# A layer's mixture of experts: each slot's step onto the sum moved behind the next slot's up, and two arms in place of four

## The chip, the cores and the metric

One core of a Trainium2 chip runs the whole layer in one launch. The metric is device time in microseconds (us) from one execution; the kernel before took 1340.64 us as the median of three runs (1333.01 to 1342.6).

## The reference

The layer takes x (256 tokens by 2048, float32). A mixer (dilated attention beside a gated recurrence) and a layer norm come first; the change does not touch them. Then come 32 experts, of which each token visits two, and a second layer norm:

```python
p_grp = jax.nn.softmax(xf @ grp_w + grp_b, axis=-1)          # 4 groups, the best one
...
top_v, top_i = lax.top_k(jax.nn.softmax(e_logits, axis=-1), TOP_K)   # its 2 best of 8 experts
weights = g_gate * top_v / jnp.sum(top_v, axis=-1, keepdims=True)
...
def expert_block(args):
    xblk, e = args
    return (jax.nn.silu(xblk @ w1[e]) * (xblk @ w3[e])) @ w2[e]
...
out = jnp.zeros((T + 1, D), x2d.dtype).at[buf_tok].add(yb * buf_w[:, None])
...
x = _layer_norm(ALPHA * x + moe, ln2_g[layer], ln2_b[layer])
```

w1 and w3 of an expert are 2048 by 512, w2 is 512 by 2048, all float32: 12 MB an expert. Experts that no token chose need not be read.

## The kernel before

The mixer takes the first 435 us. Then the routing is computed on the chip, the tokens are sorted by expert into a transposed copy (`xs`), and the experts run one after the other in 32 *slots*. Slots 0 and 1 are experts 0 and 1, whose weights are fetched before the routing is known. The other slots are filled by rank: `RHO[i]` says at which rank of token count slot `i` stands, and `bound(i)` the most tokens that a rank can have. With this data 28 experts have tokens, so slots 0 to 27 run; each is put under `tc.If(n_all > RHO[i])`. The first 25 slots (`TAIL`) are written in one loop, the others in nested conditions at the end, with the statistics of the layer norm behind each add.

A slot's 12 MB come as 12 *pieces* of 1 MB: four each of w1, w3 and w2. SyncE issues them (`load`, L757) in one fixed order into 16 homes. `advance(n)` says that n pieces have been used up, and issues what has a home then; SyncE waits there for TensorE.

One slot has these steps:
- `ahead(i + 1)` (ScalarE): copies the next slot's tokens out of `xs` into `xt`, whose two halves of 64 columns alternate.
- *up*: `up32`, `up64` or `up128` multiply the tokens by w1 and w3 (64 rows of the trace for each; the first holds up to 32 tokens and puts four products side by side on TensorE, the second up to 64 and two). ScalarE copies the result (`hs`).
- `turn`: VectorE makes the one-hot of the slot's tokens, weighted by the gate (`hot`, L902). TensorE transposes it (L912), VectorE copies it (`ohT`, L913).
- TensorE transposes `hs` (L847, L869 or L891), ScalarE applies Silu, VectorE multiplies: `gt`.
- *down* (`dn`, L925): `gt` by w2, into two banks (one for a width of 32). ScalarE copies them (`y`, L931).
- *the step onto the sum*: for each of eight blocks (two halves of the tokens, four of the columns) one matmul of `ohT` by `y` (L935) into one of three banks, and VectorE's add onto the sum (L940).

Instructions stand on each engine in the order in which the code writes them (`tc.manual_schedule()`). `expert(i)` writes a slot. Where `bound(i)` is at most 64, one arm is written; where it is more (slots 0, 1, 5, 8, 10, 11, 12, 14 and 15), `choose` writes nested conditions on the token count: slots 0 and 1 have arms for 32, 64, 128 and 256 tokens, the others for the last three. Every arm holds its own copy of the whole slot; the arm of 256 holds two passes of 128. The conditions are written so that the smaller arm comes first in the instructions of each engine, and the branch behind it (L963) jumps over the larger ones.

In slot 0 `residual` multiplies the sum by the first layer norm's gain and adds its bias: four blocks of eight small matmuls (L822) and four VectorE instructions each; two blocks are put inside the up, two behind `gt`.

## Time and profile before

| what | value |
|---|---|
| median of three runs | 1340.64 us |
| the profiled execution's own time | 1341.23 us |
| its span, first to last instruction | 1339.5 us |
| mean granted TensorE clock | 0.908 |
| TensorE busy, matmul | 1181.3 us (88%) |
| VectorE busy | 494.2 us (37%) |
| ScalarE busy | 309.1 us (23%) |
| moved by DMA | 419.76 MB, mean 313 GB/s |

Busy time is that of the whole span. [...] A trace's row of a float32 matmul of the code is two rows, so the up of 64 has 64 rows for 32 matmuls. "Idle before" is time in which the engine had nothing running, with what ended it; "issue" there means that it waited for nothing that the profile shows, among which are the branches of its own sequencer.

### The profile page before, as it was taken

The numbers are of one execution on the slowest core, as the hardware profiler recorded it, in microseconds if no ns is written. First come the engines' busy times: TensorE is split into PE (matmuls) and PEld (weight loads), VectorE is DVE, ScalarE is ACT, GpSimd is POOL, SyncE is SP. The second block draws the span as 40 slices with busy tenths as digits, with TensorE's granted clock in tenths as the row PEclk, the third lists the DMA queues.
The fourth block names the chain that finished last, engine by engine and source line by source line (L and its number), as shares of the span: only waits on it lengthen the run. The fifth ranks groups of instructions, "written<-read, shape, count | busy, mean of one in ns | idle before, by whom it ended". The sixth has DMA issues, their size and how long they took to land. (4 is left out here: it accounts for less than half of the span.)

```text
span 1339.5 us, 16366 instructions
## 1 busy us (share of the span) xinstructions
PE 1181.3 (88%) x6065; PEld 644.3 (48%) x6065; DVE 494.2 (37%) x760; ACT 309.1 (23%) x558; POOL 89.0 (7%) x91
## 2 busy tenths in 40 slices
PE   7989999999985977898889878977889999999885
PEld 6988899987874622233234222322333233333223
DVE  4779545457556423212110311121112121233336
ACT  4466444344334210101010110101101011200001
POOL 5211102130004000000000000000000000000001
PEclk9999999999996787889779899979989899999775
DMA  9634553464840779999999799899889999999992
GB/s 323 224 126 154 193 188 127 137 246 161 304 167 1 284 297 418 418 419 418 388 417 348 318 419 394 333 366 419 367 333 419 420 419 420 419 420 419 419 379 96
DMA packets 81718, 419.76 MB, mean 313 GB/s; under 512 B 7008, under 2 KB 7344, under 8 KB 38448
## 3 DMA queue, kind: packets, MB, share of 16 engines
q1 hardware_dynamic: 80384, 416.31, 78.3%
q0 software_dynamic: 912, 1.31, 0.5%
q8 instruction: 69, 1.13, 0.3%
q10 hardware_dynamic: 288, 0.48, 0.1%
q14 instruction: 65, 0.53, 0.1%
HBM read 432.75 MB, written 2.10 MB: 325 GB/s over the span
## 5 line engine op out<-in xcount | busy, mean ns | idle before, releaser
L940 DVE TENSOR_TENSOR xres<-bank,xres 128x512 f32<-128x512 f32 x224 | 146.1, 687 | 240.8 <-PE bank L935 239.7
L860 PE MATMUL bank<-ring,xt 128*64 128x512 f32 x792 | 198.3, 640 | 22.7 <-issue 22.7
L925 PE MATMUL bank<-ring,sm 128*32 128x512 f32 (+2 forms) x840 | 169.6, 646 | 28.2 <-DVE sm L872 12.1
L935 PE MATMUL bank<-sm,ar 32*128 32x512 f32 (+2 forms) x448 | 172.6, 729 | 20.4 <-DVE xres L940 10.2
L165 DVE TENSOR_TENSOR wl<-raw,wh 128x2048 fp32r<-128x2048 f32 (+1 forms) x59 | 129.7, 2207 | 101.2 <-ACT wh L164 101.2
L195 PE MATMUL bank<-xh,wl 128*128 128x256 f32 x512 | 146.3, 287 | 6.2 <-DVE wl L165 6.2
L195 PE MATMUL bank<-xh,wh 128*128 128x256 f32 x512 | 147.1, 288 | 1.2 <-ACT wh L164 1.2
L195 PE MATMUL bank<-xl,wh 128*128 128x256 f32 x512 | 146.9, 287 | 0.0
L164 ACT ACTIVATE wh<-raw 128x2048 fp32r<-128x2048 f32 (+1 forms) x59 | 107.5, 1826 | 144.2 <-PE bank L195 123.3
L838 PE MATMUL bank<-ring,xt 128*32 128x512 f32 x768 | 115.6, 714 | 21.9 <-issue 20.6
L860 PEld LDWEIGHTS bank<-ring,xt 128*64 128x64 f32 x792 | 63.8, 147 | 146.4 <-issue 146.4
L913 DVE COPY ar<-bank 128x256 f32<-128x256 f32 x28 | 11.9, 424 | 318.7 <-PE bank L912 318.7
L935 PEld LDWEIGHTS bank<-sm,ar 32*128 32x128 f32 (+2 forms) x448 | 63.9, 205 | 122.7 <-DVE xres L940 69.4
L925 PEld LDWEIGHTS bank<-ring,sm 128*32 128x32 f32 (+2 forms) x840 | 50.7, 134 | 124.9 <-issue 82.4
L195 PEld LDWEIGHTS bank<-xh,wl 128*128 128x128 f32 x512 | 99.1, 194 | 7.2 <-DVE wl L165 6.8
L195 PEld LDWEIGHTS bank<-xh,wh 128*128 128x128 f32 x512 | 99.5, 194 | 1.8 <-ACT wh L164 1.6
L195 PEld LDWEIGHTS bank<-xl,wh 128*128 128x128 f32 x512 | 99.5, 194 | 0.4
L838 PEld LDWEIGHTS bank<-ring,xt 128*32 128x32 f32 x768 | 29.2, 127 | 97.1 <-issue 95.8
L931 ACT ACTIVATE sm<-bank 128x512 f32<-128x512 f32 x47 | 28.1, 597 | 205.4 <-PE bank L925 197.4
L865 ACT ACTIVATE sm<-bank 128x512 f32<-128x512 f32 x13 | 7.8, 597 | 263.9 <-PE bank L860 263.9
L694 POOL TENSOR_TENSOR xres<-xres,offset 128x512 f32<-128x512 f32 x4 | 6.3, 1584 | 904.6 <-ACT xres L693 904.6
L882 PE MATMUL bank<-ring,xt 128*128 128x512 f32 x120 | 58.2, 642 | 2.1 <-DMA ring<-in_w_dram 2.1
(278 smaller groups left out, 1183.9 us busy)
## 6 DMA issues: line engine op xcount, KB each, us to landing
ring<-in_w_dram SPq DMA_DIRECT2D x330, 1024.0 KB
raw<-in_w_in_dram SPq DMA_DIRECT2D x39, 1024.0 KB
misc<-in_w_dram SPq DMA_DIRECT2D x22, 1024.0 KB
raw<-in_w_out_dram SPq DMA_DIRECT2D x16, 1024.0 KB
xres<-in_x_dram SPq DMA_DIRECT2D x4, 512.0 KB
out_dram<-xres SPq DMA_DIRECT2D x8, 256.0 KB
raw<-in_w_in_dram SPq DMA_DIRECT2D x4, 256.0 KB
offset<-in_ln_b_dram SPq DMA_DIRECT2D x1, 1024.0 KB
```

Of the source, the lines that this page charges most:

```text
L164: nc.scalar.activation(h[:, e], r[:, e], AF.Copy)
L165: nc.vector.tensor_tensor(out=l[:, e], in0=r[:, e], in1=h[:, e].bitcast(FT), op=OP.subtract)
L195: nc.tensor.matmul(o, lhsT=l, rhs=r, start=start, stop=stop, skip_group_check=True)
L838: nc.tensor.matmul(hp[p0:p0 + 32, :], lhsT=xt[:, j + par, i % 2 * 64:i % 2 * 64 + 32], rhs=wp(i, nm, j + par), start=j == 0, stop=j == 14)
L860: nc.tensor.matmul(hp[c * 64:c * 64 + 64, :], lhsT=xt[:, j, i % 2 * 64:i % 2 * 64 + 64], rhs=wp(i, nm, j), start=j == 0, stop=j == 15)
L865: nc.scalar.activation(hs, hp, AF.Copy)
L882: nc.tensor.matmul(hp[k], lhsT=xt[:, j, :], rhs=wp(i, nm, j), start=j == 0, stop=j == 15)
L913: nc.vector.tensor_copy(ohT, tr[:, 0:2, :])
L925: nc.tensor.matmul(yp[n * h:n * h + n, :], lhsT=gt[:, j, 0:n], rhs=w[:, c:c + 512], start=j == 0, stop=j == 3)
L931: nc.scalar.activation(y, yp, AF.Copy)
L935: nc.tensor.matmul(cp, lhsT=ohT[n * h:n * h + n, t, :], rhs=y[n * h:n * h + n, :], start=True, stop=True)
L940: nc.vector.tensor_tensor(out=a, in0=cp, in1=a, op=OP.add)
```

## The change

The step onto the sum of slot i is taken out of slot i and given to slot i + 1 as a list of eight functions, `back(i)`. Slot i + 1 puts three of them behind its up, ahead of its one-hot, and five behind `gt`, ahead of its down; slot 0 has `residual`, whole, in the place of the five. `hs` and `gt` have one buffer each. `up128` and the four arms go: the width is 64 where `bound(i)` is above 32 (in slots 0 and 1 too), and 32 elsewhere. A slot that can have more than 64 tokens has two arms: `most` (up to 64 tokens), and `all_`, which first puts down the previous slot's eight functions, then goes 64 by 64 (tokens 64 to 127; under a condition 128 to 255; and at last 0 to 63, whose step is left to the next slot). The pieces' homes are released in this last pass. Behind the loop stands `back(24)`; the slots of the tail put down their own steps at once.

```diff
--- before.py
+++ after.py
@@ -704,17 +704,15 @@
     ring = [slot(i, f"ring{i}") for i in (0, 1, 2, 3, 7, 10, 16, 17, 13, 15, 20, 14, 4, 5)] + [misc]
     R = {
         "oh": Rot([blk(0), blk(1)]),
-        "ohT": Rot([blk(2), blk(3)]),
         "sg": Rot([f[:, 256 * i:256 * i + 256].rearrange("p (j s) -> p j s", j=4) for i in (4, 5)]),
-        "hs": Rot(sm[0:2]),
-        "y": Rot(sm[0:2]),
-        "gt": Rot([t.rearrange("p (j s) -> p j s", j=4) for t in sm[2:4]]),
         "xp": Rot(bank[0:4]),
         "dn": Rot(bank[0:2]),
         "hp": Rot(bank[2:4]),
         "tr": Rot([bank[4].rearrange("p (j s) -> p j s", j=4)]),
         "yp": Rot(bank[5:8]),
     }
+    hs, gt, ys = sm[2], sm[3].rearrange("p (j s) -> p j s", j=4), sm[0:2]
+    ohTs = [blk(2), blk(3)]
     ctx.enter_context(tc.manual_schedule())
 
     wv1 = w1.rearrange("l e (q p j) f -> p (l e) q (j f)", q=4, j=4)
@@ -826,191 +824,137 @@
                 nc.vector.scalar_tensor_tensor(acc[t][:, ns], b, ALPHA, acc[t][:, ns], op0=OP.mult, op1=OP.add)
 
 
-    def up32(i, before):
+    def up32(i, step):
 
         hp = R["hp"].tile()
         for j in range(0, 16, 2):
-            if j % 4 == 0:
-                before(j // 4)
             for par in range(2):
                 for c, nm in enumerate(("1", "3")):
                     p0 = 64 * par + 32 * c
                     nc.tensor.matmul(hp[p0:p0 + 32, :], lhsT=xt[:, j + par, i % 2 * 64:i % 2 * 64 + 32],
                                      rhs=wp(i, nm, j + par), start=j == 0, stop=j == 14)
             if j % 4 == 2:
-                advance(2)
-        hs = R["hs"].tile()
-        nc.scalar.activation(hs, hp, AF.Copy)
-        ohT = turn(i, 32)
-        tr = R["tr"].tile()
-        for j in range(4):
-            nc.tensor.matmul(tr[:, j, 0:64], lhsT=hs[:, j * 128:j * 128 + 128], rhs=two, start=True, stop=True)
-        sg, gt = R["sg"].tile(), R["gt"].tile()
-        nc.scalar.activation(sg[:, :, 0:32], tr[:, :, 0:32], AF.Silu)
-        nc.vector.tensor_tensor(out=gt[:, :, 0:32], in0=sg[:, :, 0:32], in1=tr[:, :, 32:64], op=OP.mult)
-        return gt, ohT
-
-    def up64(i, before):
+                step(2)
+        return hp
+
+    def up64(i, step):
 
         hp = R["hp"].tile()
         for j in range(16):
-            if j % 4 == 0:
-                before(j // 4)
             for c, nm in enumerate(("1", "3")):
                 nc.tensor.matmul(hp[c * 64:c * 64 + 64, :], lhsT=xt[:, j, i % 2 * 64:i % 2 * 64 + 64],
                                  rhs=wp(i, nm, j), start=j == 0, stop=j == 15)
             if j % 4 == 3:
-                advance(2)
...
-    def up128(i, c, last):
-
...
-    def hot(i, n, c=0):
-
-        oh = R["oh"].tile()
+                step(2)
+        return hp
+
+    def turn(i, n, c):
+
+        oh, ohT = R["oh"].tile(), ohTs[i % 2]
         for t in range(2):
             nc.vector.tensor_scalar(oh[:, t, :].rearrange("p (r s) -> p r s", s=n),
                                     iota[:, c + 1:c + 1 + n].unsqueeze(1).to_broadcast([128, 128 // n, n]),
                                     Rs[:, t, i:i + 1], Gs[:, t, i:i + 1], op0=OP.is_equal, op1=OP.mult)
-        return oh
-
-    def turn(i, n, oh=None):
-        oh = hot(i, n) if oh is None else oh
-        ohT = R["ohT"].tile()
         tr = R["yp"].tile().rearrange("p (j s) -> p j s", j=4)
         for t in range(2):
             nc.tensor.transpose(tr[:, t, :], oh[:, t, :], ident)
         nc.vector.tensor_copy(ohT, tr[:, 0:2, :])
-        return ohT
-
-    def dn(i, gt, ohT, n, last=True):
-
-        r = 128 // n
-        yps = [R["dn"].tile() for _ in range(2)][:4 // r] if n < 128 else bank[0:4]
+
+    def chunk(i, c, step, late):
+
+        n = width(i)
+        h = 128 // n
+        hp = (up64 if n == 64 else up32)(i, step)
+        nc.scalar.activation(hs, hp, AF.Copy)
+        for f in late[0:3]:
+            f()
+        turn(i, n, c)
+        tr, sg = R["tr"].tile(), R["sg"].tile()
+        for j in range(4):
+            w = hs[:, j * 128:j * 128 + 128]
+            if n == 64:
+                nc.tensor.transpose(tr[:, j, :], w, ident)
+            else:
+                nc.tensor.matmul(tr[:, j, 0:64], lhsT=w, rhs=two, start=True, stop=True)
+        nc.scalar.activation(sg[:, :, 0:n], tr[:, :, 0:n], AF.Silu)
+        nc.vector.tensor_tensor(out=gt[:, :, 0:n], in0=sg[:, :, 0:n], in1=tr[:, :, n:2 * n], op=OP.mult)
+        for f in late[3:]:
+            f()
+        yps = [R["dn"].tile() for _ in range(4 // h)]
         for j in range(4):
             w = pieces[i, "2", j]
             for b, yp in enumerate(yps):
-                for h in range(r):
-                    c = (r * b + h) * 512
-                    nc.tensor.matmul(yp[n * h:n * h + n, :], lhsT=gt[:, j, 0:n], rhs=w[:, c:c + 512],
+                for k in range(h):
+                    nc.tensor.matmul(yp[n * k:n * k + n, :], lhsT=gt[:, j, 0:n], rhs=w[:, (h * b + k) * 512:][:, 0:512],
                                      start=j == 0, stop=j == 3)
-            if last:
-                advance(1)
-        for b, yp in enumerate(yps):
-            y = R["y"].tile()
+            step(1)
+        for y, yp in zip(ys, yps):
             nc.scalar.activation(y, yp, AF.Copy)
-            for t in range(2):
-                for h in range(r):
-                    cp = R["yp"].tile()
-                    nc.tensor.matmul(cp, lhsT=ohT[n * h:n * h + n, t, :], rhs=y[n * h:n * h + n, :], start=True, stop=True)
-                    add(cp, t, r * b + h, i >= TAIL)
-
-    def add(cp, t, n, stats):
-        a = acc[t][:, n * 512:n * 512 + 512]
-        nc.vector.tensor_tensor(out=a, in0=cp, in1=a, op=OP.add)
-        if stats:
-            nc.vector.bn_stats(bst[:, t, n, :], a)
+
+    def back(i):
+
+        n = width(i)
+        h = 128 // n
+        ohT = ohTs[i % 2]
+
+        def one(b, t, k):
+            cp = R["yp"].tile()
+            nc.tensor.matmul(cp, lhsT=ohT[n * k:n * k + n, t, :], rhs=ys[b][n * k:n * k + n, :], start=True, stop=True)
+            a = acc[t][:, (h * b + k) * 512:][:, 0:512]
+            nc.vector.tensor_tensor(out=a, in0=cp, in1=a, op=OP.add)
+            if i >= TAIL:
+                nc.vector.bn_stats(bst[:, t, h * b + k, :], a)
+        return [lambda b=b, t=t, k=k: one(b, t, k) for b in range(4 // h) for t in range(2) for k in range(h)]
+
+    def width(i):
+        return 64 if bound(i) > 32 else 32
 
     def count(i):
-        return nc.values_load(ints[0:1, i:i + 1], engines=[ET.PE, ET.Activation, ET.DVE, ET.SP], min_val=0, max_val=256,
+        c = 81 + i if i < 2 else 32 + i
+        return nc.values_load(ints[0:1, c:c + 1], engines=[ET.PE, ET.Activation, ET.DVE, ET.SP], min_val=0, max_val=256,
                               skip_runtime_bounds_check_because=WHY)
 
...
-    def expert(i):
-
...
-        def small(up, n):
+    def expert(i, late):
+
+        def most():
             if i:
                 ahead(i + 1)
-            gt, ohT = up(i, before)
-            if i == 0:
-                residual(2, 3)
-            dn(i, gt, ohT, n)
-
-        def first():
-            if i == 0:
-                residual(0, 1, 2, 3)
-
-        def wide():
-            first()
-            gt, ohT = up128(i, 0, True)
-            ahead(i + 1)
-            dn(i, gt, ohT, 128)
-
-        def huge():
-            first()
-            done[0] += 8
-            halves = [up128(i, c, False) for c in (0, 128)]
-            ahead(i + 1)
-            for c, (gt, ohT) in enumerate(halves):
-                dn(i, gt, ohT, 128, c == 1)
-        arms = [(32, lambda: small(up32, 32)), (64, lambda: small(up64, 64)), (128, wide), (256, huge)]
-        if i < 2:
-            choose(early[i], arms)
-        elif bound(i) > 64:
-            choose(count(32 + i), arms[1:])
+            chunk(i, 0, advance, late)
+
+        def more(c):
+            fetch(place(i), i % 2 * 64, c)
+            chunk(i, c, lambda n: None, [])
+            for f in back(i):
+                f()
+
+        def all_():
+            if i:
+                ahead(i + 1)
+            for f in late:
+                f()
+            more(64)
+            with tc.If(cv > 128):
+                more(128)
+                more(192)
+            fetch(place(i), i % 2 * 64, 0)
+            chunk(i, 0, advance, [])
+        evs.clear()
+        if bound(i) <= 64:
+            most()
         else:
+            cv = count(i)
+            k0 = nxt[0], done[0]
+            with tc.If(cv > 64, preferred_fallthrough_block=False) as cmp:
+                all_()
+            ends = nxt[0], done[0]
             evs.clear()
-            arms[bound(i) > 32][1]()
-            evs.clear()
+            with cmp.Else():
+                nxt[0], done[0] = k0
+                most()
+            assert ends == (nxt[0], done[0])
+        evs.clear()
 
     advance()
-    early = [count(81 + i) for i in range(2)]
     n_all = nc.values_load(ints[0:1, 80:81], min_val=2, max_val=32, skip_runtime_bounds_check_because=WHY)
     xs = []
     side = by_slot()
@@ -1026,20 +970,28 @@
     homes[:] = [spare if t is None else t for t in homes]
     advance()
     for i in range(TAIL):
-        if i < 2:
-            expert(i)
+        if i == 0:
+            expert(0, [lambda: None] * 3 + [lambda: residual(0, 1, 2, 3)])
+            continue
+        if i == 1:
+            expert(1, back(0))
             continue
         k0 = nxt[0], done[0]
         with tc.If(n_all > RHO[i]) as cmp:
-            expert(i)
+            expert(i, back(i - 1))
         ends = nxt[0], done[0]
         with cmp.Else():
             nxt[0], done[0] = k0
             evs.clear()
+            for f in back(i - 1):
+                f()
+            nc.vector.memset(ohTs[i % 2], 0.0)
             ahead(i + 1)
             advance(12)
         evs.clear()
         assert ends == (nxt[0], done[0])
+    for f in back(TAIL - 1):
+        f()
 
     for n in range(4):
         for t in range(2):
@@ -1047,7 +999,9 @@
     with ExitStack() as nest:
         for i in range(TAIL, NE):
             nest.enter_context(tc.If(n_all > RHO[i]))
-            expert(i)
+            expert(i, [])
+            for f in back(i):
+                f()
     evs.clear()
 
 
```

## Rows read from the trace of the kernel before

**Rows 1.** The page's slices: what DMA moved in 40 equal slices of the span

```profile
GB/s 323 224 126 154 193 188 127 137 246 161 304 167 1 284 297 418 418 419 418 388 417 348 318 419 394 333 366 419 367 333 419 420 419 420 419 420 419 419 379 96
```

**Rows 2.** Windows (start:end length, busy us and count by engine, clock, DMA share, GB/s)

```profile
511.51:1005.78 494.27, 426.95 (x1799) 153.85 (x1799) 99.09 (x179) 55.37 (x159) 0.00 (x0) 0.90 0.94 384
1005.78:1302.20 296.42, 274.52 (x1275) 90.75 (x1278) 81.85 (x150) 34.81 (x103) 0.00 (x0) 0.93 1.01 419
```

**Rows 3.** SyncE's waits, 511 to 1005 us (total us, times, longest)

```profile
SPq L757 <- PE bank L860: 103.8, 23, 15.6
```

**Rows 4.** Windows by slot: slots 0, 1, 3, 5, 8, 11, 20

```profile
441.82:483.51 41.69, 34.65 (x186) 18.77 (x187) 17.44 (x30) 5.66 (x17) 0.00 (x0) 0.69 0.83 328
483.51:511.51 28.00, 21.24 (x122) 7.39 (x123) 6.40 (x12) 2.38 (x7) 0.00 (x0) 0.74 0.84 342
533.41:555.26 21.85, 19.17 (x124) 6.19 (x123) 6.38 (x12) 3.28 (x11) 0.00 (x0) 0.89 1.01 418
579.36:637.08 57.72, 51.74 (x119) 22.72 (x119) 9.15 (x16) 4.71 (x13) 0.00 (x0) 0.94 1.01 418
684.76:742.91 58.15, 52.67 (x120) 22.88 (x119) 9.07 (x17) 5.70 (x17) 0.00 (x0) 0.93 0.88 344
801.13:838.19 37.06, 29.90 (x119) 10.49 (x119) 6.59 (x12) 3.08 (x8) 0.00 (x0) 0.91 0.98 396
1088.05:1116.91 28.86, 27.52 (x119) 9.47 (x118) 6.49 (x13) 3.97 (x12) 0.00 (x0) 1.00 1.01 418
```

**Rows 5.** TensorE's timeline, slot 20 (start, us, work, [idle before])

```profile
1088.05 13.96 PE L860 MATMUL bank<-ring,xt 128*64 128x512 f32 x64
1101.93 0.44 PE L912 MATMUL bank<-con,ar 128*128 128x128 f32 x2
1102.78 0.66 PE L869 MATMUL bank<-con,sm 128*128 128x128 f32 x4 [0.41 <-ACT sm L865]
1104.37 7.09 PE L925 MATMUL bank<-ring,sm 128*64 128x512 f32 x32 [0.93 <-DVE sm L872]
1111.39 5.59 PE L935 MATMUL bank<-sm,ar 64*128 64x512 f32 x16
```

**Rows 6.** VectorE's timeline behind slot 20's down

```profile
1112.55 5.16 DVE L940 TENSOR_TENSOR xres<-bank,xres 128x512 f32<-128x512 f32 x8 [8.23 <-PE bank L935]
1117.63 0.59 DVE L902 TENSOR_SCALAR ar<-con,sl 128x128 f32<-128x128 f32 x2
```

**Rows 7.** TensorE's timeline, slot 3's up and slot 9

```profile
533.41 8.42 PE L838 MATMUL bank<-ring,xt 128*32 128x512 f32 x64
...
742.91 1.92 PE L838 MATMUL bank<-ring,xt 128*32 128x512 f32 x16 [1.94 <-issue]
...
753.77 3.64 PE L925 MATMUL bank<-ring,sm 128*32 128x512 f32 x32 [0.69 <-DVE sm L850]
758.19 1.13 PE L935 MATMUL bank<-sm,ar 32*128 32x512 f32 x6 [0.78 <-ACT sm L931]
```

**Rows 8.** TensorE's timeline, slot 0 behind its up

```profile
458.65 7.23 PE L822 MATMUL bank<-ones,con 48*128 48x128 f32 x32
465.81 6.35 PE L925 MATMUL bank<-ring,sm 128*32 128x512 f32 x32
```

**Rows 9.** TensorE's branches by line (ns min/median/max, start), and its timeline around one

```profile
L963 PEldq COMPARE_BRANCH  x1: 6052/6052/6052, 630.7 to 630.7; - x1
L963 PEldq COMPARE_BRANCH  x1: 3428/3428/3428, 739.2 to 739.2; - x1
L963 PEldq COMPARE_BRANCH  x1: 5962/5962/5962, 794.3 to 794.3; - x1
789.87 5.59 PE L935 MATMUL bank<-sm,ar 64*128 64x512 f32 x16
801.13 1.12 PE L860 MATMUL bank<-ring,xt 128*64 128x512 f32 x2 [5.67 <-issue]
```

**Rows 10.** TensorE's timeline, slot 5's down

```profile
611.65 14.00 PE L925 MATMUL bank<-ring,sm 128*128 128x512 f32 x32 [0.78 <-DVE sm L892]
```

50 lines of the change are left out of this document (removed).

## The prediction

> **What bounds the kernel now.** I read the page's slices first [rows 1]: the last two thirds are the expert slots, and DMA moves 419 GB/s there at best, with dips. Windows show where the dips lie [rows 2, 4]: 328 and 342 GB/s in slots 0 and 1, 384 over slots 2 to 16 (511.5 to 1005.8 us), 419 over slots 17 to 27. So up to 1005.8 the transfers wait for somebody: in that stretch SyncE, which issues every piece, waits longest for TensorE, 103.8 us for the ups of 64 alone [rows 3]. There are 16 homes of 1 MB, a slot needs 12, and a home comes free only when TensorE has read it. From 1005.8 on DMA is full and sets the pace: 12 MB at 419 GB/s are 12.58/0.419 = 30.0 us a slot, while TensorE does a slot of width 64 in 28.86 us [rows 4]. Hence the rule of the sum: what TensorE's chain gains or loses before slot 17 moves everything behind it by as much (as long as DMA still has its 41 us of idle time to give: (419 - 384)/419 of 494 us); what it gains or loses after is mostly swallowed by DMA.
>
> The slot table [rows 4] and TensorE's timeline [rows 5 to 7] give the slots' classes. This data has two wide slots (5 and 8, 57.7 and 58.2 us), choosing slots that take the arm of 64 (10, 11, 12, 14, 15; about 37 us), plain ones of 64 (28.9 us) and of 32 (about 22 us). Slots 0 and 1 choose 32 now: the down of slot 0 is 128*32 [rows 8]. [...]
>
> **The change, part by part.** *The branch stays.* There are still nine choosing slots; the small arm still stands first and still has to jump over the large one, which holds four passes of 64 in place of three of 128. The skip of two passes of 128 and the skip of three cost the same in the rows (6.05 and 5.96), so I take no change: 5.7 us idle and 2.4 us of clock behind each, as now. Below nothing would need the sequencer to run further ahead (a rival).
>
> *The seam of a plain slot of 64.* Now it is: up ends, 2.37 us to the down (0.44 and 0.66 us of transposes, idle for 0.41 and 0.93), down 7.09, the eight steps onto the sum 5.59 [rows 5]; without up and down 28.86 - 13.96 - 7.09 = 7.8 us. After: three of the previous slot's steps behind the up, the one-hot's turn, the transposes, the other five steps, the down. The design hides 1.3 us of idle time. But on VectorE `late[0:3]` puts three adds ahead of the one-hot (L902), which now is made early, during the up. An add starts 1.16 us after its step (1111.39 to 1112.55) and eight take 5.16 us, 0.65 each [rows 5, 6]: the third ends at about 1.16 + 2 x 0.70 + 0.65 = 3.2, the one-hot (0.59) at 3.8, the turn begins at 3.9 us, while TensorE's three steps ended at 2.1: 1.8 us idle. Turn and transposes to 5.0; five steps of 0.70, the fourth and fifth of them held until the bank's add, queued behind the gate's multiply, frees it (no more than 0.1 here): 8.4 us. So +0.5 a slot. Bounds: TensorE's work alone, 5.6 + 1.1 = 6.7 (-1.1); with the next up also waiting for the copy behind the down (0.78 us, as the step waits in [rows 7]), 9.2 (+1.4). I take +0.5, for the order of the queues is written out. Six slots of 64 lie before slot 17: **+3 us**.
>
> *The seam of a slot of 32.* Now 21.85 - 8.42 - 3.64 = 9.8 us in slot 3 (a down of 32 is 3.64) [rows 4, 7]: some 2.6 to the down, 0.78 until the copy lets the steps begin, 6.4 of steps, held by adds. The 0.78 goes, and the steps run partly under the transposes; by the same queues 8.3 to 8.8. I take -1.4 (at a fallen clock the steps of now are longer), bounds -0.5 and -3. Seven such slots (2, 3, 4, 6, 7, 9, 13): **-10 us**.
>
> *Slots 0 and 1 lose the arm of 32.* An up of 64 costs 13.96 against 8.42, a down 7.09 against 3.64 [rows 5, 7]. Slot 1: 16.4 (with the clock's 2.4) + 8.4 + 7.1 + 5.7 = 37.5 against 28.0: +9.5. Slot 0 also moves half of `residual` from inside the up to the seam: two of its four parts take 7.23 us there now, four then some 13.4; 13.96 + 1.5 (transposes) + 13.4 + 10 (down at the fallen clock, as 6.35 stands for 3.64 now) + 5.6 = 44.5 against 41.7 [rows 4, 8], its own steps now falling to slot 1: +3. **+12.5 us**, bounds 8 and 16.
>
> *The wide slots.* A pass of 128 costs what two of 64 cost: slot 5's down begins 32.3 us after the slot (579.36 to 611.65) against 2 x 16.3, and takes 14.0 against 2 x 7.1 [rows 4, 5, 10]. What comes on top: the previous slot's steps stand bare ahead of the up (0.8 + 6.5), the first pass's own steps bare behind its down (5.5), a second seam of 2.4, and a branch over two more passes between the passes. That branch meets idle DMA: the first pass releases nothing, so of 16 homes four go on loading (10 us). The rows have 3.43 us for a branch while DMA idled, with 1.94 us idle TensorE [rows 7, 9]. Sum: 7.3 + 16.4 + 2.4 + 7.1 + 5.5 + 1.9 + 15.2 + 2.4 + 7.1 = 65.3 against 57.7 and 58.2: **+14.5 us** for both, 19 with a branch of 6.05. `more`'s four fetches on ScalarE lie under the bare steps (6.5 and 5.5 us); without that cover, at the 0.78 us that the copy in [rows 7] makes TensorE wait, 3 us each.
>
> *SyncE* issues the same pieces in the same order; in the wide slots all releases come in the second pass. No extra DMA, and nothing on POOL. *Behind slot 24* its steps stand bare (5.6 us, with the eight statistics behind them as now); DMA paces slots 25 to 27 [rows 2], which hides it; bare 5.6.
>
> **The sum.** +12.5 + 14.5 - 10 + 3 = +20 us at slot 17; from there DMA carries it to the end. The profiled execution was 1341.2 us (span 1339.5, 1.7 around it), the median of the runs 1340.6: 1361 us.
>
> **Rivals.**
> *A: the branch gets hidden (faster).* The arm now ends in the down, which waits for no add, where it ended in steps that wait for banks; a sequencer that runs far ahead would take the jump under the down. For it: at 794.3 the last step's bank wait had just ended. Against: the branch began only 1.1 us before TensorE ran dry (794.3; the steps end at 789.87 + 5.59 = 795.5) [rows 9]. Price: at seven arms of 64 5.3 us and 2.3 us of clock, 53 us; with +20 that is -33, and DMA's idle time (41 us) could give it: 1308 us. It decides from a lead of more than 20/7 = 3 us over now. [...] Chance 0.1.
> *B: the seams hide as meant.* If the one-hot is not held up, each seam of 64 is 6.7 us and each of 32 about 7.5: 6 x -1.1 and 7 x -2.6 in place of +3 and -10, that is -25 against -7, and the sum is +2 to +5: 1345 us. For it: idle time is there to hide. Against: VectorE's written order. Chance 0.2.
> *C: the clock falls in the new seams.* A slot behind a branch, 5.67 us idle, has 0.91, a plain one with 0.41 and 0.93 us idle keeps 1.00 [rows 4, 5, 9]. The new 1.8 us in one piece lies between. If each of some 15 seams loses 1.7 us (half of a fallen stretch like those that cost an up 2.4): +25, 1386 us. Chance 0.2.
>
> **How the numbers follow.** Forecast 0.5 (1350 with one term at its low bound, 1374 with all at their high ones), A 0.1, B 0.2, C 0.2. The range from 1343 to 1386 leaves out A and the far side of C. About 1% (13 us) is what a measurement here can tell from no change. Slower by more than that (over 1354): nearly all of the forecast and C, a little of B: 0.7; within: most of B and the forecast's low edge: 0.2; faster: A, 0.1.
>
> **What would show it.** Right: ups of 64 in slots 0 and 1 and slot 1 near 37 us; wide slots at 65 with a branch in the middle; after each choosing slot still 5 to 6 us idle before the up; in plain slots TensorE idle ahead of the turn (the wait for the one-hot, behind three adds); slots of 64 near 29.4; DMA at 419 GB/s again from slot 17 on, with all of it some 20 us later. Wrong: branches under 2 us, one-hots that run before the adds, wide slots under 60, or slots behind 17 that DMA no longer paces.

## The result, and the profile after

The kernel after takes 1349.68 us (median of 17 runs), the kernel before 1339.8 beside it (17 runs): ratio 1.0085, 95% interval 1.0062 to 1.0108. Timed a second time beside the experiments the ratio was 1.0119 (1.0077 to 1.0161). So the change costs about 1%, some 10 to 14 us, where +20 was forecast. The profiled execution is 1346.55 us with a span of 1344.8. The predicted time and the direction came out near, but not by the predicted way, as the traces show.

In the kernel after, the up of 64 is L845, the up of 32 L834, the one-hot L855, its turn L860, the transposes L876 (64) and L878 (32), the down L888, the step onto the sum L902 with its add L904, the issue of a piece L755. L947 is the branch of a choosing slot, L936 the one between the two passes and the third and fourth.

**Where TensorE's chain went.** Windows by slot of the kernel after, in order slots 0, 1, 3, 5, 8, 12, 20 (columns as in [rows 4]; slot 12 stands for 11, whose up has a stall of its own after the change, told in the last section):

```profile
442.10:480.70 38.60, 34.53 (x168) 18.65 (x169) 12.25 (x21) 7.01 (x20) 0.00 (x0) 0.87 0.79 307
480.70:511.40 30.70, 27.42 (x118) 10.16 (x118) 6.42 (x12) 3.08 (x8) 0.00 (x0) 1.00 1.00 397
535.90:558.90 23.00, 20.02 (x130) 6.24 (x126) 6.29 (x12) 2.38 (x7) 0.00 (x0) 0.78 1.01 419
577.80:647.40 69.60, 59.84 (x240) 20.42 (x240) 13.02 (x24) 8.03 (x20) 0.00 (x0) 0.90 0.72 295
689.50:757.00 67.50, 58.81 (x237) 19.87 (x236) 13.30 (x24) 7.92 (x20) 0.00 (x0) 0.92 0.73 300
849.30:880.00 30.70, 27.49 (x122) 10.26 (x125) 6.42 (x12) 2.89 (x8) 0.00 (x0) 1.00 1.01 417
1078.50:1107.10 28.60, 27.22 (x122) 9.29 (x120) 6.42 (x12) 3.98 (x13) 0.00 (x0) 1.00 1.01 420
```

A choosing slot that takes the arm of 64 now lasts 30.7 us at a granted clock of 1.00, which is full speed, where it lasted about 37 at 0.91 [rows 4]. Summed over all slots, slot 17 starts at 991.2 us where it started at 1005.8 [rows 2]: TensorE's chain gained 14.6 us, and the forecast was a loss of 20. The differences by class, slot by slot against the kernel before, are: slots 0 and 1 -0.4 us, the two wide slots +21.3, slots of 32 -14.8, slots of 64 -21.0.

The gain in the slots of 64 is in the branch. First the branch behind slot 11 (ns, start), then TensorE's timeline there (start, us, work, [idle before]):

```profile
L947 PEldq COMPARE_BRANCH  x1: 6111/6111/6111, 842.3 to 842.3; - x1
```

```profile
839.61 3.65 PE L888 MATMUL bank<-ring,sm 128*64 128x512 f32 x16
843.10 1.89 PE L888 MATMUL bank<-misc,sm 128*64 128x512 f32 x8
844.81 1.89 PE L888 MATMUL bank<-ring,sm 128*64 128x512 f32 x8
849.29 1.94 PE L845 MATMUL bank<-ring,xt 128*64 128x512 f32 x8 [2.59 <-ACT xt L805]
```

The jump still takes 6.11 us, as in [rows 9], but it begins at 842.3, 4.4 us before the down ends (844.81 + 1.89 = 846.70). Before, it began 1.1 us before the steps ended. TensorE is idle for 2.59 us instead of 5.67, and starts again 0.9 us after the jump's end, as in [rows 9]. Over the seven choosing slots that leave by the small arm, the idle time behind them was 36.8 us and is 15.7 (21.1 less).

**Where the transfers went.** Three windows, first of the kernel before, then of the kernel after (columns as in [rows 2]; the last number is GB/s):

```profile
511.50:770.00 258.50, 229.85 (x984) 86.53 (x986) 54.56 (x98) 29.95 (x84) 0.00 (x0) 0.89 0.96 392
770.00:990.00 220.00, 182.65 (x760) 62.35 (x758) 39.34 (x72) 22.32 (x67) 0.00 (x0) 0.90 0.91 373
990.00:1270.00 280.00, 262.61 (x1199) 87.60 (x1193) 75.16 (x137) 35.33 (x103) 0.00 (x0) 0.96 1.01 419
```

```profile
511.50:770.00 258.50, 223.88 (x1167) 75.73 (x1168) 60.94 (x116) 31.56 (x89) 0.00 (x0) 0.91 0.86 353
770.00:990.00 220.00, 191.87 (x864) 69.38 (x864) 48.00 (x89) 25.68 (x78) 0.00 (x0) 0.95 1.01 418
990.00:1270.00 280.00, 258.61 (x1149) 87.84 (x1149) 73.40 (x134) 33.85 (x100) 0.00 (x0) 0.93 1.01 419
```

DMA's idle time in a window is reckoned as (419 - GB/s)/419 of its length, 419 being the rate of both kernels from 990 to 1270. Before: 16.7 us up to 770 and 24.2 from there to 990, 40.9 in all. After: 40.7 and 0.5, 41.2 in all. The idle time has not become less; it has moved into the wide slots. SyncE's waits in the kernel after show it (us in total, times, longest, 511 to 1005 us, as in [rows 3]):

```profile
SPq L755 <- PE bank L845: 103.0, 19, 34.5
```

The total is that of [rows 3], 103.8, but its longest wait is 34.5 us, where 15.6 was the longest. In a wide slot both passes read all twelve pieces, so a home comes free in the second pass only: piece 6.4 (slot 6, fifth piece) is issued at 627.7, when 6.3 has landed at about 610.6; piece 9.4 at 737.4, with 9.3 down at about 721.5. Both times DMA has nothing to do for 17 to 19 us: no weights move from 610.2 to 628.7 and from 721.0 to 738.4, which is 35.8 of the 41.2 us. A window of the first hole, and the page's slices with both (163 and 178 GB/s):

```profile
610.00:627.00 17.00, 13.94 (x48) 4.61 (x46) 5.75 (x10) 2.53 (x6) 0.00 (x0) 0.90 0.01 2
```


```profile
GB/s 317 227 126 145 200 178 137 126 251 160 289 171 16 282 357 394 418 418 163 418 419 178 421 418 418 418 417 418 416 419 420 419 420 419 420 418 419 420 301 96
```

So the first piece of slot 17 lands at 977.2 us, 8.2 later than before, though TensorE reaches slot 17 14.6 us earlier. From 738.4 on DMA runs without a stop up to the last piece, and from slot 17 on a slot takes 29.99 us (slot 27 starts at 1291.09, ten slots behind 991.22), the 30.0 us that the prediction worked out for 12 MB, where it took 28.4 before. TensorE waits for the last piece of all until 1309.4, where it waited until 1307.6, first in the kernel before, then in the kernel after:

```profile
1307.61 1.94 PE L925 MATMUL bank<-ring,sm 128*32 128x512 f32 x8 [2.13 <-DMA ring<-in_w_dram]
```

```profile
1309.40 1.94 PE L888 MATMUL bank<-ring,sm 128*32 128x512 f32 x8 [1.42 <-DMA ring<-in_w_dram]
```

Behind the last piece the tail is 3.5 us longer (1344.8 - 1309.4 = 35.4 against 1339.5 - 1307.6 = 31.9), nearly all of it in one row, TensorE's idle time before the closing products, first of the kernel before, then of the kernel after:

```profile
1322.28 7.19 PE L677 MATMUL bank<-ones,con 48*128 48x128 f32 x32 [1.76 <-PEq L1047]
```

```profile
1327.41 7.20 PE L677 MATMUL bank<-ones,con 48*128 48x128 f32 x32 [5.10 <-issue]
```

### The profile page after: what moved, and what is told of

Same layout as the page of the kernel before. It is cut to its first block, busy times and chain, and to the rows that moved or that the text cites. A ratio compares the mean times of both kernels' runs of the same rounds, so it can differ in the third digit from the quotient of the medians.

```text
span 1344.8 us, 16840 instructions
## 1 busy us (share of the span) xinstructions
PE 1189.5 (88%) x6293; PEld 645.8 (48%) x6293; DVE 502.5 (37%) x782; ACT 314.5 (23%) x574; POOL 88.1 (7%) x91
## 5 line engine op out<-in xcount | busy, mean ns | idle before, releaser
L904 DVE TENSOR_TENSOR xres<-bank,xres 128x512 f32<-128x512 f32 x240 | 153.7, 685 | 525.9 <-PE bank L902 525.4
L845 PE MATMUL bank<-ring,xt 128*64 128x512 f32 x1152 | 277.1, 610 | 24.6 <-ACT xt L805 8.6
L902 PE MATMUL bank<-sm,ar 64*128 64x512 f32 (+1 forms) x480 | 184.2, 768 | 16.3 <-DVE xres L904 8.2
L888 PE MATMUL bank<-ring,sm 128*64 128x512 f32 (+1 forms) x904 | 177.8, 632 | 12.2 <-DMA ring<-in_w_dram 6.4
L845 PEld LDWEIGHTS bank<-ring,xt 128*64 128x64 f32 x1152 | 94.4, 141 | 188.1 <-issue 172.2
L165 DVE TENSOR_TENSOR wl<-raw,wh 128x2048 fp32r<-128x2048 f32 (+1 forms) x59 | 129.6, 2203 | 103.8 <-ACT wh L164 103.8
L902 PEld LDWEIGHTS bank<-sm,ar 64*128 64x128 f32 (+1 forms) x480 | 64.1, 215 | 115.3 <-DVE xres L904 56.3
L888 PEld LDWEIGHTS bank<-ring,sm 128*64 128x64 f32 (+1 forms) x904 | 50.5, 133 | 132.2 <-issue 106.5
L868 ACT ACTIVATE sm<-bank 128x512 f32<-128x512 f32 x30 | 17.9, 597 | 363.2 <-PE bank L845 263.5
L892 ACT ACTIVATE sm<-bank 128x512 f32<-128x512 f32 x49 | 29.3, 597 | 282.3 <-PE bank L888 282.3
L834 PE MATMUL bank<-ring,xt 128*32 128x512 f32 x648 | 87.8, 634 | 8.0 <-issue 6.8
L834 PEld LDWEIGHTS bank<-ring,xt 128*32 128x32 f32 x648 | 23.8, 116 | 65.8 <-issue 51.2
L805 ACT ACTIVATE xt<-xs 128x128 f32 (+2 forms) x196 | 46.9, 310 | 27.1 <-PEq L936 14.9
```

Source lines behind the costliest of these rows:

```text
L165: nc.vector.tensor_tensor(out=l[:, e], in0=r[:, e], in1=h[:, e].bitcast(FT), op=OP.subtract)
L805: nc.scalar.activation(xt[:, 4 * q:4 * q + 4, to:to + n], xs[q][:, :, at], AF.Copy)
L834: nc.tensor.matmul(hp[p0:p0 + 32, :], lhsT=xt[:, j + par, i % 2 * 64:i % 2 * 64 + 32], rhs=wp(i, nm, j + par), start=j == 0, stop=j == 14)
L845: nc.tensor.matmul(hp[c * 64:c * 64 + 64, :], lhsT=xt[:, j, i % 2 * 64:i % 2 * 64 + 64], rhs=wp(i, nm, j), start=j == 0, stop=j == 15)
L868: nc.scalar.activation(hs, hp, AF.Copy)
L888: nc.tensor.matmul(yp[n * k:n * k + n, :], lhsT=gt[:, j, 0:n], rhs=w[:, (h * b + k) * 512:][:, 0:512], start=j == 0, stop=j == 3)
```

## The experiments

Theory H: what counts is the time for which the transfers stand still, since homes are held by the second pass. Rival P: what counts is TensorE's own longer work in the wide slots. A third question, theory L, was whether the sequencer's lead at the branch comes from the down having nothing to wait for.

**Each half of the change alone.** `wide128` is the kernel after with one pass of 128 tokens in the wide slots, as in the kernel before; the moved step and the lost arm of 32 stay.

```diff
-                all_()
+                with tc.If(cv > 128, preferred_fallthrough_block=False) as big:
+                    all_()
+                ...
+                with big.Else():
+                    wide()      # one up, one down of 128, its own steps bare behind it
```

> The changed kernel, in which slots with 65 to 128 tokens go in one pass of 128 again (their own steps bare, the following slot then adds zeros); the deferral of all other steps is kept. Theory H (the two holes in the transfers, about 609 to 629 and 720 to 740 us of the changed kernel's trace, in which a wide slot's first pass frees no home, set the time; TensorE's chain has about 35 us to spare behind them): both holes go, the last weights land some 30 us earlier, about 1308 us (1300 to 1318), ratio to the kernel before near 0.977, and slot 17 starts near 979 us. Rival P (TensorE's chain sets the time throughout): only the second seam, the branch between the passes and its clock go, some 6 us for each of two slots: about 1337 us.

Measured: 1319.34 us, ratio to the kernel before 0.9864 (0.9837 to 0.9892). Its windows, as above:

```profile
511.50:770.00 258.50, 234.80 (x1036) 91.62 (x1030) 64.40 (x116) 29.84 (x84) 0.00 (x0) 0.92 0.95 390
770.00:990.00 220.00, 195.06 (x865) 71.15 (x862) 49.32 (x93) 26.49 (x77) 0.00 (x0) 0.95 1.01 418
990.00:1270.00 280.00, 253.40 (x1147) 85.39 (x1149) 80.41 (x146) 33.17 (x99) 0.00 (x0) 0.93 1.01 419
```

The two long holes are gone: 390 GB/s up to 770, 18.4 us of idle time to 990. The time lies 1.3 us over H's range and 18 under P's figure. The moved step alone (with the lost arm of 32) is a gain of 1.4%, and the kernel beats both. The wide slots still take 62.7 and 62.0 us, 5.0 and 3.9 more than before.

`before_two_passes` is the other half: the kernel before, with the tokens of an arm over 64 taken by passes of 64.

```diff
+            for c in (64, 0):           # in a new function, twice()
+                fetch(place(i), i % 2 * 64, c)
+                gt, ohT = up64(i, lambda q: None, c, c == 0)
+                dn(i, gt, ohT, 64, c == 0)
...
-        arms = [..., (128, wide), (256, huge)]
+        arms = [..., (128, twice), (256, huge)]
```

> The kernel before, in which slots with 65 to 128 tokens go in two passes of 64, each with its own steps behind its down; homes are freed in the second pass; nothing is deferred. Theory H (time is the later of the two chains): the kernel before is bound by TensorE up to slot 17, so this adds what the passes add there, some 7.5 us a wide slot, and the holes in the transfers lie where DMA would have waited anyway: about 1355 us. Rival (the holes cost their idle time whatever TensorE does): two holes of 20 us, about 1380 us.

Measured: 1356.05, ratio 1.0157 (1.0103 to 1.0211): the 1355 that was expected, not the rival's 1380. On the chip of these runs, with 1337.5 before, the four corners are: neither 1337.5, step moved 1319.3, two passes 1356.05, both 1351.7 (`after_again`, the kernel after itself).

> The changed kernel as it is, for a second profile beside the others and to see what differs from run to run. If the tail's second stall (TensorE idle 5.1 us before the gain's products at L677, where the kernel before has 1.8) comes from the place of the code, it is here again; if it was chance, the gap is near 2 us. The two holes in the transfers are expected again at the two wide slots, 18 to 20 us each. Time 1344 to 1356 us.

The halves alone are -18.1 and +18.6, which adds to nothing; together they cost +14.2. The tail's second stall came back in `after_again` (4.81 us idle before L677) and is 1.8 to 2.0 in the two halves, so some 3 us of the missing 14 are the tail's. Most of the rest is in the transfers. In the profiled executions the missing part is 16.9 us of span, and 13.0 of it is DMA's idle time (table below): the halves change that by -22.5 and +12.9, both together by +3.4. The kernel before has 24.2 us of idle DMA time behind 770, with the step moved there is 0.5; that a part of a hole's lateness goes into such time where there is some is argued from this, not tested.

**The sequencer's lead.** In `own_step_bare` a choosing slot makes the first of its own steps behind its own down again, and only the other seven move.

```diff
             chunk(i, 0, advance, late)      # small arm; the same behind the large one
+            if bound(i) > 64:
+                back(i)[0]()
...
-            expert(i, back(i - 1))
+            expert(i, rest(i - 1))      # back(i - 1) without its first step
```

> The changed kernel, in which slots that choose do the first of their own eight steps bare behind their down (it waits for the copy there); the other seven stay with the next slot. Theory L (TensorE's sequencer got 4.4 us ahead in the changed kernel because nothing behind the down's start waits): the step's wait holds the branch back, TensorE stands idle 5 us or more behind each choosing slot of 64 again in place of 1.8 to 2.6, and the clock falls there: the chain up to slot 17 gets some 20 to 30 us longer, so slot 17 starts near 1015 us. Rival (the branch got cheaper for its place in the code): the idle time stays at 2 to 3 us. As to the time: by theory H (DMA sets it after the holes) at most 10 us of this shows, 1345 to 1360 us; by rival P all of it, about 1373 us.

TensorE's timeline behind slot 15 and the branch there:

```profile
998.81 1.89 PE L888 MATMUL bank<-ring,sm 128*64 128x512 f32 x8
1000.62 1.12 PE L902 MATMUL bank<-sm,ar 64*128 64x512 f32 x2
1006.91 1.98 PE L845 MATMUL bank<-ring,xt 128*64 128x512 f32 x4 [5.16 <-issue]
```

```profile
L953 PEldq COMPARE_BRANCH  x1: 5987/5987/5987, 1000.6 to 1000.6; - x1
```

One step, which waits for ScalarE's copy of the down (999.97 to 1000.57), is enough: the branch starts as that copy and the down end, the idle time is back to 5.0 to 6.0 us in all but one of the slots (10.54 there), the next ups take 16 to 17 us again, and slot 17 starts 46.7 us later than in the kernel after. Theory L is shown. The time is 1376.91, ratio 1.0303 (1.0253 to 1.0353), 25 us more than the kernel after: more than the 10 that H allowed, and less than the chain lost. It lies near the 1373 of rival P, though the chain lost 46.7 us, not the 20 to 30 that this figure stood on.

**Holes or work.** The first attempt, `wide128_late_release`, told nothing of H:

```diff
-                if j % 4 == 3:
-                    advance(2)       # and advance(1) in the down
+            advance(12)              # all twelve behind the down
```

> wide128 (the changed kernel with one pass of 128 in the two wide slots; 1319 us), in which a wide slot frees all its twelve homes at the end of its down in place of as they are read. TensorE has not one product more. Theory H (the hole in the transfers while a wide slot holds its homes is what the two passes of 64 cost): the holes of the changed kernel come back, some 20 us at each wide slot, and the time comes near the changed kernel's less its tail's second stall: 1338 to 1347 us. Rival P (the extra products, seam and branch of the second pass cost it): nothing changes, 1317 to 1323 us.

It moves the place of the issue in SyncE's order, but SyncE waits for the last reader of a home, which is unchanged: 6.4 to 6.11 go out between 590.9 and 610.7, in `wide128` between 591.2 and 612.6. 1323.21, ratio 0.9881 (0.9848 to 0.9915).

`two_halves_side_by_side` computes what the kernel after computes, both halves of 64 of a wide slot piece by piece, so that each piece is read by both and then free.

```diff
+                for m, hp in zip(at, hps):          # the two halves, inside the loop over pieces
+                    for c, nm in enumerate(("1", "3")):
+                        nc.tensor.matmul(hp[c * 64:c * 64 + 64, :], lhsT=xt[:, j, m:m + 64], rhs=wp(i, nm, j), ...)
```

> The changed kernel, in which 65 to 128 tokens still go as two halves of 64, but side by side: both ups read a piece before its home is freed, then both downs; homes are freed as they are read. TensorE has the same ups and downs as in the changed kernel. Theory H: no hole, about as wide128: 1315 to 1325 us. Rival P (two passes of 64 cost because they are two): some 1335 to 1345 us.

Measured: 1336.99 (11 runs), ratio 0.9998 (0.9979 to 1.0016), with 372 GB/s up to 770: better than the kernel after by some 13 us and worse than `wide128` by 18. By its time it lies in P's band, by its transfers between the two (the profiled execution is the fastest of the eleven, 1330.43).

Then each suspect was added to `wide128` by itself. `wide128_homes_held` reads every piece once more behind the down, with products of 32 columns:

```diff
+            for k, (nm, q) in enumerate(order12):
+                w = pieces[i, nm, q]
+                nc.tensor.matmul(cp[0:32, 0:32], lhsT=w[:, 0:32], rhs=w[:, 0:32], start=k == 0, stop=k == 11)
+            advance(12)
```

> As wide128 (one pass of 128 tokens in slots 5 and 8), but behind the down of these two slots twelve more products of 32 columns read each of the slot's twelve weight pieces once more, so that each home has its last reader there, as the second pass of 64 has it in the kernel after; the extra products are never used and cost TensorE well under 2 us a slot. Theory H (the transfers that stand still while the homes are held are what the two passes cost): piece 6.4 is issued at about 629 us instead of 590.9, a slice of the page with under 200 GB/s comes back at about 615 and another at about 725, piece 17.0 lands about 25 us later than wide128's 947.8, and the time is about 1340 us (1333 to 1348). Theory P (TensorE's own longer work in the two slots, 7 and 6 us a slot, is what they cost): 1319 to 1325 us.

SyncE's longest waits, 511 to 1005 us, and the windows:

```profile
SPq L755 <- PE bank L972: 83.4, 2, 42.9
```

```profile
511.50:770.00 258.50, 223.19 (x958) 86.92 (x962) 57.85 (x104) 27.68 (x78) 0.00 (x0) 0.89 0.80 329
770.00:990.00 220.00, 190.65 (x886) 70.08 (x879) 47.68 (x90) 26.66 (x80) 0.00 (x0) 0.97 1.01 418
```

The extra products take 0.95 us a slot, and the time is 1360.5, ratio 1.019 (1.0108 to 1.0273): 41 us more than `wide128`. P falls as the only cause. H was under-sized at 1340: 6.4 goes out at 636.2, the stops are longer than in the kernel after (26.5 and 23.9 us), and piece 17.0 lands 40.9 later than in `wide128`.

`wide128_more_products` and `wide128_few_products` add work instead, before the down, and hold no home on purpose:

```diff
+            for k in range(32):      # 8 in few_products
+                nc.tensor.matmul(extra, lhsT=gt[:, k % 4, :], rhs=xs[0][:, k % 4, :], ...)
```

> As wide128, but ahead of the down of slots 5 and 8 TensorE makes 32 more products of 512 columns, about 7 us a slot, from operands that are long there and into a bank that nobody reads; homes come free as in wide128. Theory H (held homes cost, TensorE's work does not): 1319 to 1325 us, with no slice under 200 GB/s between 520 and 990 us. Theory P (TensorE's longer work costs): wide128 plus 13, 1329 to 1335 us.

> wide128_more_products with 8 extra products in place of 32: the profile of that run showed that the 32 took 27.73 us in slot 5 (64 rows of the profile, 0.43 us each), four times the 7 us that were meant, so 8 take about 7 us, which is what the kernel after spends more than wide128 in each wide slot. They stand ahead of the down, so the slot's last four homes come free 7 us later and the first eight as before. Theory H (only a stop of the transfers costs; 7 us more of TensorE's work, with eight of twelve homes free in time, makes none): 1319 to 1326 us. Theory P (TensorE's work costs as it is, with or without held homes): wide128's 1319.3 plus 14, 1330 to 1336 us.

With 32 products the dose was four times too large (27.73 us in slot 5: a product is two rows, and a row of this width takes 0.43 us, as in the down of [rows 10], 14.00 us for 32): 1379.81, ratio 1.0309 (1.0247 to 1.0371). With 8 it is as meant:

```profile
619.39 7.13 PE L967 MATMUL bank<-xs,sm 128*128 128x512 f32 x16 [0.78 <-DVE sm L964]
```

```profile
511.50:770.00 258.50, 230.31 (x964) 90.57 (x966) 58.09 (x104) 28.14 (x79) 0.00 (x0) 0.91 0.88 357
770.00:990.00 220.00, 196.88 (x840) 70.84 (x834) 44.97 (x84) 25.69 (x78) 0.00 (x0) 0.88 1.00 408
```

1348.41, ratio 1.0075 (1.0043 to 1.0106): 14.3 us of added work cost 29, against H's 0 to 7 and P's 14. So H falls as the only cause too, and P's size was half of what came. The windows say how: with the work ahead of the down, the slot's last four homes and all later ones come free later. SyncE waits 40.1 us in all for the wide slots' downs where it waited 26.3 in `wide128`, 121.3 for those of the other slots where it waited 58.6, and the transfers stand still for 44.0 us where they stood 18.4. Added work and held homes reach the time by the same road. About 4 us of the 29 lay ahead of slot 0 in the profiled run, and a lower clock from 770 to 990 (0.88 against 0.95) comes with it; how much that adds was not separated.

The stops lie elsewhere than in the kernel after, though. Here pieces move at the full rate while the kernel after has its first hole, and the first stop comes behind the wide slot (the last number is GB/s):

```profile
612.00:628.00 16.00, 14.59 (x38) 6.51 (x37) 1.72 (x3) 1.40 (x5) 0.00 (x0) 1.00 1.02 423
645.00:656.00 11.00, 6.97 (x26) 1.89 (x29) 2.63 (x5) 0.66 (x4) 0.00 (x0) 0.69 0.02 4
```

In the kernel after DMA moves 421 GB/s from 645 to 656.

**The seams.** `wide128_early_one_hot` makes the one-hot on VectorE ahead of the three adds.

```diff
+        oh = hot(i, n, c)            # tensor_scalar, before the late steps
         for f in late[0:3]:
             f()
-        turn(i, n, c)
+        turn(i, oh)
```

> wide128 with the one-hot put on VectorE ahead of the three adds, so that it is made during the up. The prediction's step (the one-hot waits behind the adds and leaves TensorE idle ahead of its turn, 1.4 us in slots of 64 and 2.2 us in slots of 32): that idle time goes to some 0.2 and 0.8 us. As DMA is full from 770 us on in wide128, only slots 1 to 7 count, 6 to 8 us of TensorE's chain: 1311 to 1316 us, ratio to the kernel before about 0.981. If the idle time only moves behind the turn (the copy of the transposed one-hot, or the wait for the scores' copy), 1318 to 1320 us.

The seam of slot 20 in the kernel after, then a seam of 64 in this kernel:

```profile
1092.30 1.98 PE L902 MATMUL bank<-sm,ar 64*128 64x512 f32 x6
1095.66 0.58 PE L860 MATMUL bank<-con,ar 128*128 128x128 f32 x2 [1.38 <-DVE ar L855]
1096.08 0.60 PE L876 MATMUL bank<-con,sm 128*128 128x128 f32 x4
1096.61 3.62 PE L902 MATMUL bank<-sm,ar 64*128 64x512 f32 x10
1100.17 7.09 PE L888 MATMUL bank<-ring,sm 128*64 128x512 f32 x32
```

```profile
1067.73 1.98 PE L906 MATMUL bank<-sm,ar 64*128 64x512 f32 x6
1069.65 0.44 PE L863 MATMUL bank<-con,ar 128*128 128x128 f32 x2
1069.92 0.60 PE L880 MATMUL bank<-con,sm 128*128 128x128 f32 x4
1070.45 3.63 PE L906 MATMUL bank<-sm,ar 64*128 64x512 f32 x10
```

The wait for the one-hot, 1.38 us a slot, is gone, and behind a slot of 32 2.22 became 0.77. The time is 1320.02, ratio 0.9874 (0.9847 to 0.99), the same as `wide128`, not the 1311 to 1316 that was expected: from 505 to 1290 us 34.3 us of waits for the one-hot are gone, the ups' waits for pieces went from 7.9 to 35.4, and the transfers' windows are the same 390 and 418 GB/s.

**What orders all of them.** DMA's idle time from 511.5 to 1270 us, worked out from the three windows as above (419 - GB/s, over 419, times the window), beside the span of the profiled execution (which lies up to some 7 us off the median of its kernel's runs):

| kernel | GB/s in the three windows | idle, us | span, us | span - idle |
|---|---|---|---|---|
| wide128 | 390, 418, 419 | 18.4 | 1315.7 | 1297.3 |
| wide128_early_one_hot | 390, 418, 419 | 18.4 | 1318.0 | 1299.6 |
| wide128_late_release | 380, 409, 419 | 29.3 | 1326.5 | 1297.2 |
| two_halves_side_by_side | 372, 417, 419 | 30.1 | 1328.6 | 1298.5 |
| before | 392, 373, 419 | 40.9 | 1339.5 | 1298.6 |
| after | 353, 418, 419 | 41.2 | 1344.8 | 1303.6 |
| after_again | 348, 418, 419 | 44.3 | 1346.8 | 1302.5 |
| wide128_few_products | 357, 408, 419 | 44.0 | 1343.4 | 1299.4 |
| before_two_passes | 364, 390, 412 | 53.8 | 1353.7 | 1299.9 |
| wide128_homes_held | 329, 418, 419 | 56.0 | 1356.5 | 1300.5 |
| own_step_bare | 350, 382, 408 | 69.4 | 1375.2 | 1305.8 |
| wide128_more_products | 334, 372, 417 | 78.4 | 1377.5 | 1299.1 |

Spans that differ by 62 us come to within 3 us of 1299.5, once DMA's idle time is taken off; the three that lie higher (1302.5 to 1305.8) are those with the longer stall in the tail. This is the account that stands: the time is the transfers' work plus the time for which they stand still. A part of it is bookkeeping: all the kernels move the same weights, so the table shows that little else differs from kernel to kernel, ahead of the slots and behind the last piece, and not why a stop comes. For that there are the runs above: a home that comes free late, be it for a late last reader (`wide128_homes_held`) or for added work (`wide128_few_products`), makes the transfers stand. In the kernel after the place of the stops speaks for the last reader: both end when the second pass reads the first pieces, as in `wide128_homes_held`, and none stands behind the wide slot, where added work alone lengthens one (12.0 us, against 5.0 in `wide128`). How long they would be if the second pass came with less work ahead of it was not separated.

## Why the prediction was right or wrong

The direction was right and the time lies in the range; about half of the +20 came. That the time came so near is luck: two of its steps failed in opposite ways and largely cancelled. A time over 1354, to which the prediction gave 0.7, did not come, and rival B's 1345 lies nearer than the forecast's 1361, though what B rests on did not come either.

- **"The branch stays: 5.7 us idle and 2.4 us of clock behind each."** This failed. The branch's price stayed (6.11 us), its start moved: a lead of 4.4 us over the down's end in place of 1.1, idle time of 1.8 to 2.6 us, and ups of 13.95 where they were 16.3 to 16.9 (slot 11's apart). The forecast's 2.4 us of clock are what those ups took above a plain one's 13.96 [rows 5], 2.3 to 2.9 us: behind the branch at 794.3 the granted clock was 0.50 from 799.0 to 805.8 us. Rival A had named the mechanism and the point from which it decides, a lead of more than 3 us over now; the lead grew by 3.3. Of a down of 7.09 us, 4.4 us lay behind the branch's start; how much further ahead the sequencer could run, no run shows. The row of before was read as a limit of the sequencer, 1.1 us, when it was the wait of the last steps; `own_step_bare` shows that.
- **"The first pass releases nothing ... DMA idled."** The holes were foreseen and costed only as a cheaper branch. That a stop of the transfers costs by itself, where they have no idle time left to make it up, was the missing step. It follows from the prediction's own first part (16 homes, released by TensorE), and the +14.5 for the wide slots had no term for it. `wide128_homes_held` shows that a stop of this kind alone costs 41 us.
- **"What TensorE's chain gains or loses before slot 17 moves everything behind it by as much."** This failed. The chain gained 14.6 and the end moved by +5.3 in the profiled pair. `wide128_early_one_hot` shaved the seams of `wide128` for nothing; `own_step_bare` lost 46.7 at slot 17 and 25 in time. The end follows DMA's idle time, and the chain that ran ahead of its pieces gained nothing by it: from slot 17 to the last piece TensorE takes 318.2 us where it took 301.8. Rival A's 1308 us fails by the same step, though its mechanism came; `wide128` at 1319 is nearest to it.
- **The wide slots, +14.5**, came to +21.3. In slot 5 (69.6 against 65.3) the excess is in TensorE's idle time: 3.45 us on entry where 0.8 was taken, since the large arm is now the one that is jumped to (a branch of 5.12 us at 575.9, where the longest before was 0.33 at 578), and 3.06 between the passes where 1.9 was taken (branch of 3.50), with 1.0 on the previous slot's steps. The passes cost what was said: 25.1 and 25.0 us.
- **Slots 0 and 1, +12.5**, came to -0.4. Slot 1's 37.5 held 8.1 us for the branch and its clock and came to 30.7. Slot 0's 44.5 came to 38.6; it took the down at the fallen clock (10; measured 8.93), 13.4 for the residual products (11.78) and 5.6 for steps that the same paragraph had said fall to slot 1: an error of counting.
- **The seams.** Of 64: slot 20 lasts 28.60 us, which leaves 7.6 without its up of 13.90 and its down of 7.09, where 8.4 was forecast and 7.8 was before; the wait for the one-hot behind the adds is there, 1.38 us in place of 1.8. Rival B, seams that hide as meant, did not hold in the kernel after; the early one-hot makes them so in `wide128` and gains nothing. Slots of 32: -14.8 where -10 was forecast; behind a slot of 32 the idle time before the turn is 2.2 to 2.3 us, as in slot 3:

```profile
546.24 0.58 PE L860 MATMUL bank<-con,ar 128*128 128x128 f32 x2 [2.22 <-DVE ar L855]
```

  Rival C came in part. 1.38 us of idle time leaves slot 20 at a clock of 1.00, but in slots 3, 7 and 10, with 2.2 to 2.3 us, the granted clock fell to 0.50 in the seam (547.9 to 558.2, 677.7 to 687.9 and 793.7 to 803.9 us; 0.78, 0.78 and 0.86 over the slot), and seam and down together took some 4.2 us longer than in slots 4 and 14 (16.1 against 11.8 us in slots 3 and 4). Slots 4 and 14 kept 1.00 with the same idle time, and with the early one-hot (0.77 us of it) slots 3 and 7 still had slow downs (6.22 and 5.98 us against 3.64): that this idle time is the cause is not shown.
- **The tail**, costed at nothing, has a second stall: 5.10 us before the closing products against 1.76, twice in this kernel and not in either half of the change. In it, from 1324.8 to 1325.7, a packet of 16384 bytes runs on the instruction queue, the second since the jump at 1320.2; the kernel before has one by the time the products start. So it goes with a second such packet (last section). That the place of the code decides this was not tested.

## What to carry to other kernels

Where a ring of buffers ties a stream of transfers to one engine, sum the stream's idle time before and after the change, look where its stops lie, and ask of each edit when it frees each buffer for the last time; here a second pass over the same weights held them for a whole pass, and SyncE's longest wait went from 15.6 to 34.5 us. A jump over a large arm left TensorE idle for 1.8 to 2.6 us behind work that waited for nothing, and for 5.0 to 6.0 (10.54 once) with a single waiting instruction ahead of it. An engine's gain counts only as far as the transfers can follow (14.6 us gained at slot 17 here, and an end 5.3 us later), so halves of a change that cancel on paper (-18 and +19) need not cancel together (+14).

## What was not expected of the hardware

- The sequencer ran 4.4 us ahead of TensorE into a branch behind a down of 32 rows that waits for nothing; with one waiting product behind such a down the lead was gone, and the idle time behind slot 15 went from 1.95 to 5.16 us.
- The jump's price goes with what DMA does meanwhile. Windows over three jumps: in the kernel after between the passes (3.50 us from 618.2), in `wide128` at the end of slot 5 (3.82 from 633.9), and the same jump in `wide128_homes_held` (6.13 from 642.2), where the held pieces had just been issued (the last number is GB/s):

```profile
618.00:622.00 4.00, 1.28 (x4) 0.29 (x2) 2.20 (x5) 0.13 (x1) 0.00 (x0) 1.00 0.02 4
```

```profile
634.00:638.00 4.00, 1.74 (x5) 0.43 (x3) 2.34 (x4) 0.28 (x2) 0.00 (x0) 1.00 0.41 166
```

```profile
642.20:648.30 6.10, 1.77 (x5) 0.46 (x3) 2.35 (x4) 0.30 (x2) 0.00 (x0) 1.00 1.02 420
```

  At 4 GB/s it took 3.5 us, at 166 3.8, at 420 6.1. In each of the three jumps a packet of 16384 bytes runs on the instruction queue (q8 of the page) and ends 1.4 to 1.5 us before the jump does. It starts 0.9, 1.3 and 3.7 us after the jump begins, so the 2.3 to 2.6 us more behind a full stream of weights lie in the wait for this packet to start. The kernels before and after have 22 jumps of TensorE's sequencer of over 3 us, and each has such a packet, which ends 1.3 to 1.5 us before the jump does: in those of 3.4 to 3.8 us it starts 0.9 to 1.0 us after the jump's start, in the two of 5.12 us 2.6 to 2.7, in those of 5.8 to 6.3 us 3.3 to 3.9. That the jump waits for the packet is read from these times, not tested.
- A jump can be followed by a second stall. In slot 11 of the kernel after TensorE does four rows of the up behind the jump and stands idle again, with no semaphore waited for; a packet of 16384 bytes runs on the instruction queue from 814.0 to 815.1:

```profile
811.58 1.08 PE L845 MATMUL bank<-ring,xt 128*64 128x512 f32 x4 [2.57 <-DMA ring<-in_w_dram]
816.36 15.39 PE L845 MATMUL bank<-ring,xt 128*64 128x512 f32 x60 [3.70 <-issue]
```

  The up lasts 20.17 us by it and by the fall of the clock that follows (0.50 from 814.2 to 821.0). (The 2.57 us ahead of it are the jump, which ends at 810.7; the slot's first piece had landed at 793.2.) In `after_again` the stall is there too (3.74 us), and the 10.54 us of `own_step_bare`, at the same slot, hold two such packets.
